# Other slots for the small tiles of the SSM, and its samples' transfers issued by POOL

## The chip, the cores and the metric

The kernel runs on one core of one Trainium2 chip. Its time is the device time of one execution in microseconds (us); several executions are timed and their median is given. In the profile, PE is TensorE (PEld its weight loads), DVE is VectorE, ACT is ScalarE, POOL is GpSimd and SP is SyncE. A suffix q, as in SPq, means that engine's sequencer, which issues DMAs and waits for semaphores.

## What is computed

One inference step of a hybrid decoder layer, in fp32, for one prompt of 1024 tokens with 16 meta tokens ahead of it and for 8 sample rows that each have a state of their own. Cut to what matters here:

```python
h = h + 0.5 * swiglu(rmsnorm(h, n1), w1g, w1u, w1d)
u = rmsnorm(h, nm) @ w_in
q, fz, iv, g, z, xbc, dt_raw = jnp.split(u, SPLITS, axis=-1)
# HGRN2: 4 heads of 128, a gated linear recurrence, S_t = diag(f_t) S_{t-1} + k_t v_t^T
o_hg, s_hg = run_segments(hgrn2_chunked, HG_CHUNK, segs, s_hg, silu(q), kk, iv, logf)
# Mamba-2 (SSM): 8 heads of 64, 2 groups, state 128; causal conv, then a chunked scan
xbc_act, conv_buf = causal_conv(xbc, s_conv, conv_w, conv_b)
dt = jax.nn.softplus(dt_raw + dt_bias)
#   per step: h_t = exp(dt_t A) h_{t-1} + dt_t x_t B_t^T ;  y_t = h_t C_t + D x_t
y, s_ssm = run_segments(functools.partial(ssd_chunked, a_neg=a_neg), SSM_CHUNK, segs, s_ssm, xs, dt, bm, cm)
mix = jnp.concatenate([o_hg, yz], axis=-1) @ w_out
h = h + mix
h = h + 0.5 * swiglu(rmsnorm(h, n2), w2g, w2u, w2d)
```

The outputs are the final norm of the prompt's and the samples' rows and all new states: SSM and HGRN states for the prompt, and for each of the 8 samples an SSM state (8 heads × 64 × 128, 256 KB) and an HGRN state (4 heads × 128 × 128).

## The kernel before

**Data and products.** Activations lie transposed: 128 partitions are features, the 1048 columns are tokens (1040 of the prompt, 8 samples). Every projection is made of three fp32r matmuls, high × high, high × low and low × high (`mm3`, L144 to L146). A weight tile of 128×512 is loaded raw by SP (`weights`, L126, from the pool "r"), its high part is made by ACT (L138) and its low part by DVE (L139).

**Stages in order.** FFN 1, with an order written out by hand; the mixer; FFN 2, by hand again. The mixer is `ssm_project` (projection, conv, and `ssm_decay` with the decays of all tokens), then the SSM scan and the SSM samples together, then four HGRN heads, each with projection, scan, samples and output, and the SSM gate (`ssm_gate`, L1263) and norm (`ssm_norm`, L1279, L1283) in between, then `out_proj`. In the mixer a scheduler decides the order of the instructions on each engine from the program's order and from which buffers are free; each engine then runs its list strictly in order. A DMA issue is an instruction in the list of the engine that issues it, so what stands behind a waiting issue waits too.

**Buffers.** `SLOTS = {"u": 30, "s": 8}`: 30 slots of kind "u" and 8 of kind "s", each 128×1056 fp32. `Pack` takes a slot and hands out pieces of it for small tiles. The pool "r" has 8 buffers of 128×512 for raw weights; the samples' states and rows take theirs from the same pool (`K.raw()`).

**The scan, `ssm_scan`.** Nine chunks (`CT`): eight of 128 tokens and one of 16. For each chunk c, three slots of kind "s" are taken. `mt` receives the cumulated decay of each head, broadcast over all partitions (`cumd`, L1118); ACT makes the decay matrix from it (Relu L1144, Exp L1145); DVE multiplies it with C·B (L1147). A pack `tk` holds `ec` (from `cumd` too, L1125), `bt` and `cbm`. `xx` holds x times dt and x times the decay. PE's L1151 gives the part inside the chunk, L1157 the part from the state; DVE adds them (L1158, L1159, L1162) and updates the state (L1170, L1171). Between the chunks' matmuls the scheduler places matmuls of the next projection. During the scan, four of the eight "s" slots belong to others: `K.st` (the small tiles of the decays), `ssm_samples`' `ex` and its `st`, and the pack of the state buffers.

**SSM samples, `ssm_samples`.** For each of 8 samples, SP loads the state (L1224, 512 rows of 512 B) and the row of B and C broadcast to 128 partitions (L1225, 128 rows of 2 KB). POOL multiplies the state with its decay (L1226) and adds the update in two halves (L1230, L1231). DVE reduces it with C (L1238, four), and SP stores the state (L1239). `skip` (L1249) closes the samples.

**HGRN samples.** In each head, twice four samples: load of the states and of v broadcast (L1492, L1493, by SP), three operations on POOL (L1494 to L1496), one matmul per sample on PE (L1499), and a store (L1500, by SP).

POOL's other DMAs are the seven small parameter loads at the start (L761).

Of the kernel before, what the change touches and what calls it, by code (L numbers as in the profile page):

```python
# [17 lines left out]
P = 128  # L18
D = 1024
KT = D // P  # L20
# [756 lines left out]
def constants_mix(K, a):  # L777
    nc = K.nc
    cst = K.const
    K.st = K.pack()  # L780

    K.tri = cst.tile([P, P], F32, name="tri")
    nc.gpsimd.affine_select(K.tri, K.ones[1], pattern=[[1, P]], compare_op=ALU.is_ge, fill=0.0, base=0, channel_multiplier=-1)

    K.mid = cst.tile([P, 32], U8, name="mid")
    for r in range(0, P, 32):
        nc.gpsimd.tensor_copy(K.mid[r : r + 32], K.ident[r : r + 32, r : r + 32])
    K.mask = {}
    for m in LEVELS[:5]:
        nb = 64 // m  # L790
        f = K.sml.tile([P, 64], F32, tag="mf", name=K.uid("mf"))
        fv = f.rearrange("p (b i) -> p b i", i=m)
        on = K.ones[1][:, :64].rearrange("p (b i) -> p b i", i=m)

        nc.gpsimd.affine_select(fv, on, pattern=[[-2 * m, nb], [0, m]], compare_op=ALU.is_ge, fill=0.0, base=0, channel_multiplier=1)
        nc.gpsimd.affine_select(fv, fv, pattern=[[2 * m, nb], [0, m]], compare_op=ALU.is_ge, fill=0.0, base=m - 1, channel_multiplier=-1)
        u = cst.tile([P, 16], U8, name=f"mask{m}")
        for r in range(0, P, 32):
            nc.gpsimd.tensor_copy(u[r : r + 32], f[r : r + 32, r // 2 : r // 2 + 16])
        K.mask[m] = u  # L800


    l0, l1 = K.pc["lb_logits"][:, 0:4], K.pc["lb_logits"][:, 4:8]
    e = K.st.tile([P, 12])
    nc.vector.tensor_max(e[:, 8:12], l0, l1)
    nc.vector.tensor_sub(e[:, 0:4], l0, e[:, 8:12])
    nc.vector.tensor_sub(e[:, 4:8], l1, e[:, 8:12])
    nc.scalar.activation(e[:, 0:8], e[:, 0:8], AF.Exp)
    nc.vector.tensor_add(e[:, 8:12], e[:, 0:4], e[:, 4:8])
    nc.vector.reciprocal(e[:, 8:12], e[:, 8:12])  # L810
    K.lb = cst.tile([P, 4], F32, name="lb")
    K.oml = cst.tile([P, 4], F32, name="oml")
    nc.vector.tensor_mul(K.lb, e[:, 0:4], e[:, 8:12])
    nc.vector.tensor_scalar(K.oml, K.lb, -1.0, 1.0, ALU.mult, ALU.add)

    K.dtb = K.st.tile([P, 8])
    nc.sync.dma_start(K.dtb, a["dt_bias"].to_broadcast([P, 8]))
    K.an = K.st.tile([P, 8])
    nc.sync.dma_start(K.an, a["a_log"].to_broadcast([P, 8]))
    nc.scalar.activation(K.an, K.an, AF.Exp)  # L820
    nc.vector.tensor_scalar_mul(K.an, K.an, -1.0)
    K.dcol = K.st.tile([P, 4])
    for hf in range(2):
        nc.sync.dma_start(K.dcol[64 * hf : 64 * hf + 64, :], a["d_skip"].rearrange("l (j f) -> f l j", f=2)[hf].to_broadcast([64, 4]))

    K.sel16 = cst.tile([16, 8], F32, name="sel16")
    s2 = K.sml.tile([16, 8], F32, tag="s2", name="s2", bufs=1)
    nc.gpsimd.affine_select(K.sel16, K.ones[1][:16, :8], pattern=[[-1, 8]], compare_op=ALU.is_equal, fill=0.0, base=0, channel_multiplier=1)
    nc.gpsimd.affine_select(s2, K.ones[1][:16, :8], pattern=[[-1, 8]], compare_op=ALU.is_equal, fill=0.0, base=-8, channel_multiplier=1)
    nc.gpsimd.tensor_add(K.sel16, K.sel16, s2)  # L830
# [137 lines left out]
def ssm_project(K, a, o):  # L968

    nc = K.nc  # L970
# [1 line left out]
    pc = K.pc  # L972


    rw = K.st.tile([P, KT, 8])
    nc.sync.dma_start(rw, wv[:, :, C_DT : C_DT + 8])
    wd = K.sml.tile([P, KT, 16], F32R, tag="wdt", name="wdt", bufs=1)
    nc.scalar.copy(wd[:, :, 0:8], rw)
# [14 lines left out]
    ps = K.psm()  # L993
    for k in range(8):
        nc.tensor.transpose(ps[:, 24 * k : 24 * k + 24], sc[:, k * P : (k + 1) * P], K.ident[:24, :24])
    sb = K.st.tile([P, 8, 8, 3])
    nc.vector.tensor_copy(sb.rearrange("p k b j -> p (k b j)"), ps[:, :192])

    K.xs = []
# [41 lines left out]
def ssm_decay(K, dtT):  # L1041

    nc = K.nc
# [2 lines left out]
    for c, (t0, n) in enumerate(CT):  # L1046
        nc.tensor.matmul(ps[:n, 8 * c : 8 * c + 8], dtT[:, t0 : t0 + n], K.sel16, start=True, stop=True)
    nc.tensor.matmul(ps[:8, 72:80], dtT[:, TP:T], K.sel16, start=True, stop=True)
    st = K.st

    def small(name):
        return st.tile([P, 80])

    K.dt = small("dt")
    x = small("dtx")
# [43 lines left out]

    pt = K.psm()  # L1100
    nc.tensor.transpose(pt[:72, :P], K.cum[:, 0:72], K.ident)
    ct = st.tile([72, P])
    nc.vector.tensor_copy(ct, pt[:72, :P])
    K.cumd = K.dram.tile([72, P], F32, name="cumd")
    nc.sync.dma_start(K.cumd, ct)
# [1 line left out]

def ssm_scan(K, a, o):
    nc = K.nc
    st = K.st  # L1110
    hts = K.pack()
    hbuf = [hts.tile([P, 512]) for _ in range(2)]
    xs, B, C = K.xs[0:4], K.xs[4:6], K.xs[6:8]
# [68 lines left out]
def ssm_samples(K, a, o):  # L1182

    nc = K.nc
    xs, B, C = K.xs[0:4], K.xs[4:6], K.xs[6:8]

    ex = K.pack()
    expd = ex.tile([8, 4, P])
    o8 = ex.tile([8, 512])
    nc.gpsimd.memset(o8, 1.0)  # L1190
    nc.gpsimd.affine_select(expd.rearrange("h j (f p) -> h j f p", f=2), o8.rearrange("h (j f p) -> h j f p", j=4, f=2), pattern=[[-2, 4], [-1, 2], [0, 64]], compare_op=ALU.is_equal, fill=0.0, base=0, channel_multiplier=1)
    st = K.pack()
    pd = K.psm()
    nc.tensor.transpose(pd[:8, 0:8], K.dt[:8, 72:80], K.ident[:8, :8])
    nc.tensor.transpose(pd[:8, 8:16], K.da[:8, 72:80], K.ident[:8, :8])
    dT = st.tile([8, 16])
    nc.vector.tensor_copy(dT, pd[:8, 0:16])
    pe = K.psm()
    for j in range(4):
        nc.tensor.matmul(pe[:, 16 * j : 16 * j + 16], expd[:, j], dT, start=True, stop=True)  # L1200
    pev = pe[:, 0:64].rearrange("p (j s b) -> p j s b", j=4, s=2)
    dec = st.tile([P, 4, 8])
    dx = st.tile([P, 4, 8])
    ys = st.tile([P, 4, 8])
    nc.scalar.activation(dec, pev[:, :, 1], AF.Exp)
    for j in range(4):
        nc.vector.tensor_mul(dx[:, j], pev[:, j, 0], xs[j][:, TP:T])
    pr = K.psm()
    for i in range(4):
        nc.tensor.transpose(pr[:8, i * P : (i + 1) * P], (B + C)[i][:, TP:T], K.ident)  # L1210
    br = st.tile([8, 512])
    nc.scalar.copy(br, pr[:8])
    bd = K.dram.tile([8, 512], F32, name="sbd")
    nc.sync.dma_start(bd, br)
    sv = a["state_ssm"].rearrange("l b (j f) p n -> l b (f p) j n", f=2)
    ov = o["ssm_sample"].rearrange("l b (j f) p n -> l b (f p) j n", f=2)

    state = {}

    def update(b):  # L1220
        sb = K.raw().rearrange("p (j n) -> p j n", j=4)
        rw = K.raw()
        rows = rw.rearrange("p (i n) -> p i n", i=4)
        nc.sync.dma_start(sb, sv[0, b])  # L1224
        nc.sync.dma_start(rw, bd[b : b + 1, :].to_broadcast([P, 512]))  # L1225
        nc.gpsimd.tensor_mul(sb, sb, dec[:, :, b : b + 1].broadcast_to([P, 4, P]))  # L1226
        for g in range(2):
            j2 = slice(2 * g, 2 * g + 2)
            up = K.t(2 * P).rearrange("p (j n) -> p j n", j=2)
            nc.gpsimd.tensor_mul(up, rows[:, g, None].broadcast_to([P, 2, P]), dx[:, j2, b : b + 1].broadcast_to([P, 2, P]))  # L1230
            nc.gpsimd.tensor_add(sb[:, j2], sb[:, j2], up)  # L1231
        state[b] = sb, rows

    def output(b):
        sb, rows = state.pop(b)
        junk = K.t(4 * P).rearrange("p (j n) -> p j n", j=4)
        for j in range(4):
            nc.vector.tensor_tensor_reduce(junk[:, j], sb[:, j], rows[:, 2 + j // 2], 1.0, 0.0, ALU.mult, ALU.add, ys[:, j, b : b + 1])  # L1238
        nc.sync.dma_start(ov[0, b], sb)  # L1239

    def sample(b):
        if b < NS:
            update(b)
        if b > 0:
            output(b - 1)

    def skip():
        for j in range(4):
            nc.vector.scalar_tensor_tensor(xs[j][:, TP:T], xs[j][:, TP:T], K.dcol[:, j : j + 1], ys[:, j], ALU.mult, ALU.add)  # L1249

    return [lambda b=b: sample(b) for b in range(NS + 1)] + [skip]
# [98 lines left out]
def hgrn_scan(K, a, o, hd, u):  # L1350

    nc = K.nc
# [136 lines left out]
    def samples(b0):  # L1489
        sb = K.raw().rearrange("p (b v) -> p b v", b=4)  # L1490
        vb = K.raw().rearrange("p (b v) -> p b v", b=4)
        nc.sync.dma_start(sb, a["state_hgrn"][0, b0 : b0 + 4, hd].rearrange("b k v -> k b v"))  # L1492
        nc.sync.dma_start(vb, vd[b0 : b0 + 4].partition_broadcast(P))  # L1493
        nc.gpsimd.tensor_mul(sb, sb, qs[:, 8 + b0 : 12 + b0, None].broadcast_to([P, 4, P]))  # L1494
        nc.gpsimd.tensor_mul(vb, vb, qs[:, 16 + b0 : 20 + b0, None].broadcast_to([P, 4, P]))
        nc.gpsimd.tensor_add(sb, sb, vb)  # L1496
        for i in range(4):
            b = b0 + i
            nc.tensor.matmul(po8[:, 16 + b : 17 + b], sb[:, i], qs[:, b : b + 1], start=True, stop=True)  # L1499
        nc.sync.dma_start(o["hgrn_sample"][0, b0 : b0 + 4, hd].rearrange("b k v -> k b v"), sb)  # L1500

    K.jobs += [lambda: samples(0), lambda: samples(4)]
    pieces.append((po8, 1024, 24))
# [423 lines left out]
```

## Time and profile before

| | us |
|---|---|
| median of three runs | 2042.24 |
| lowest and highest of them | 2039.06 and 2136.24 |
| the profiled execution, its time | 2041.44 |
| its span in the profile | 2039.7 |
| PE busy | 1962.5 (96%) |
| DVE busy | 1469.2 (72%) |
| ACT busy | 825.5 (40%) |
| POOL busy | 154.5 (8%) |

The profile is one execution, taken by the chip's profiler. Engines run side by side, so the shares do not add up to one. Busy shares are means over stages with different limits; the views by window and by wait tell what holds a given stage. The page's slices show where engines are busy, in tenths, in 40 slices of 51 us each; the scan lies in the 17th to 19th.

```profile
PE   6999999999999999979999999989999999999997
DVE  7777777777788586597453656877777777768973
POOL 3000000000002210231020111200000000000000
DMA  6233333335966621263120345224332333587851
```

### The profile page before, as it was taken

How to read it: one execution, taken by the hardware profiler on the slowest of the kernel's cores; microseconds unless marked ns; L12 is line 12 of the kernel's file. 1: busy time of each engine (PE TensorE's matmuls, PEld its weight loads, DVE VectorE, ACT ScalarE, POOL GpSimd, SP SyncE). 2: the span in 40 equal slices, each digit the busy share in tenths (PEclk: the TensorE clock that was granted, in tenths of full speed). 3: DMA queues.
4: the chain of work that ended last, by engine and by line, in shares of the span. 5: the costliest groups of instructions: out<-in, count | busy, mean ns of one | idle time of the engine just before them, and what ended most of it. 6: DMA issues, size and time to landing. Idle time of an engine off the chain costs nothing.

```text
span 2039.7 us, 40744 instructions
## 1 busy us (share of the span) xinstructions
PE 1962.5 (96%) x16647; PEld 1916.8 (94%) x16647; DVE 1469.2 (72%) x2439; ACT 825.5 (40%) x1530; POOL 154.5 (8%) x197
## 2 busy tenths in 40 slices
PE   6999999999999999979999999989999999999997
PEld 5999999999999999968989889989999999999997
DVE  7777777777788586597453656877777777768973
ACT  6522222223534553564534435742222222354352
POOL 3000000000002210231020111200000000000000
PEclk8999999999999999999999999999999999999999
DMA  6233333335966621263120345224332333587851
GB/s 212 76 103 90 101 104 94 96 94 179 315 211 213 183 82 33 90 189 92 50 75 11 107 124 182 72 70 113 93 109 80 103 102 96 161 239 238 265 176 61
DMA packets 323890, 259.32 MB, mean 127 GB/s; under 512 B 17584, under 2 KB 299440, under 8 KB 323696
## 3 DMA queue, kind: packets, MB, share of 16 engines
q1 hardware_dynamic: 323464, 256.68, 41.6%
q8 instruction: 131, 2.15, 0.4%
q14 instruction: 55, 0.45, 0.1%
q0 software_dynamic: 224, 0.04, 0.0%
q10 hardware_dynamic: 16, 0.00, 0.0%
HBM read 191.26 MB, written 65.47 MB: 126 GB/s over the span
## 4 chain that ended last, share of the span: by engine, by line
PE 82%; DVE 9%; DMA 3%; issue 2%; ACT 2%; SPq 0%; POOL 0%; DVEq 0%; ACTq 0%; POOLq 0%
PE acc L144 25%; PE acc L146 25%; PE acc L145 25%; DMA r<-in_w_ffn_up_dram 1%; DVE u L299 1%; DMA s<-in_x_prompt_dram 1%; DMA s<-cumd 1%; DVE ws L369 1%; PE mis L1462 0%; DVE u L578 0%; DVE t L449 0%; DVE ws L640 0%; PE mis L1420 0%; DVE s L664 0%; PE mis L1151 0%
## 5 line engine op out<-in xcount | busy, mean ns | idle before, releaser
L144 PE MATMUL acc<-u,ws 128*128 128x262 f32 (+2 forms) x4504 | 1321.1, 293 | 24.0 <-DVE t L463 6.5
L146 PE MATMUL acc<-u,ws 128*128 128x262 f32 (+2 forms) x4504 | 1316.3, 292 | 3.2 <-DVE ws L369 3.2
L145 PE MATMUL acc<-u,ws 128*128 128x262 f32 (+2 forms) x4504 | 1314.3, 292 | 4.2 <-DVE u L299 3.4
L144 PEld LDWEIGHTS acc<-u,ws 128*128 128x128 f32 x4504 | 857.7, 190 | 29.1 <-issue 10.4
L145 PEld LDWEIGHTS acc<-u,ws 128*128 128x128 f32 x4504 | 860.4, 191 | 8.2 <-DVE u L299 4.9
L146 PEld LDWEIGHTS acc<-u,ws 128*128 128x128 f32 x4504 | 855.4, 190 | 5.4 <-DVE ws L369 4.2
L369 DVE TENSOR_TENSOR ws<-r,ws 128x512 fp32r<-128x512 f32 x308 | 212.6, 691 | 78.8 <-ACT ws L365 78.7
L365 ACT CAST ws<-r 128x512 fp32r<-128x512 f32 x308 | 174.2, 616 | 4.9 <-DVE r L361 4.8
L484 ACT ACTIVATE t<-t 128x524 f32<-128x524 f32 x47 | 30.3, 645 | 305.8 <-DVE t L449 305.8
L361 DVE TENSOR_TENSOR r<-r,r 128x512 f32<-128x512 f32 x176 | 121.2, 691 | 13.2 <-DMA r<-in_w_ffn_up_dram 11.4
L205 POOL TENSOR_TENSOR t<-t,t 128x262 f32<-128x262 f32 x56 | 55.3, 998 | 778.8 <-ACT t L204 778.8
L461 ACT ACTIVATE t<-t 128x524 f32<-128x524 f32 x41 | 26.4, 644 | 204.5 <-DVE t L449 204.5
L578 DVE TENSOR_TENSOR u<-u,u 128x1048 fp32r<-128x1048 f32 (+1 forms) x84 | 97.8, 1167 | 9.2 <-ACT u L574 9.2
L139 DVE TENSOR_TENSOR ws<-r,ws 128x512 fp32r<-128x512 f32 x88 | 65.9, 759 | 42.4 <-ACT ws L138 42.1
L449 DVE TENSOR_TENSOR t<-t,u 128x524 f32<-128x524 f32 x135 | 91.0, 702 | 2.9
L664 DVE SCALAR_TENSOR_TENSOR s<-acc,s 128x524 f32<-128x524 f32 (+1 forms) x88 | 55.8, 650 | 41.5 <-PE acc L146 40.8
L574 ACT CAST u<-u 128x1048 fp32r<-128x1048 f32 (+1 forms) x84 | 83.4, 996 | 1.6 <-DMA u<-hd 1.6
L635 ACT CAST ws<-u 128x512 fp32r<-128x512 f32 (+1 forms) x72 | 42.2, 587 | 101.1 <-DVE u L630 93.1
L640 DVE TENSOR_TENSOR ws<-r,ws 128x512 fp32r<-128x512 f32 (+1 forms) x84 | 57.6, 698 | 31.0 <-ACT ws L635 31.0
L138 ACT CAST ws<-r 128x512 fp32r<-128x512 f32 x88 | 54.0, 618 | 55.0 <-PE acc L146 27.9
L635 ACT CAST ws<-r 128x512 fp32r<-128x512 f32 (+1 forms) x84 | 47.5, 582 | 70.1 <-DVE r L630 35.2
L454 ACT COPY t<-acc 128x524 f32<-128x524 f32 (+1 forms) x46 | 26.6, 579 | 106.0 <-PE acc L146 106.0
(381 smaller groups left out, 1897.8 us busy)
## 6 DMA issues: line engine op xcount, KB each, us to landing
hd<-s SPq DMA_DIRECT2D x170, 262.0 KB
u<-hd SPq DMA_DIRECT2D x64, 524.0 KB
r<-in_w_ffn_down_dram SPq DMA_DIRECT2D x128, 256.0 KB
r<-in_w_ffn_gate_dram SPq DMA_DIRECT2D x88, 256.0 KB
r<-in_w_ffn_up_dram SPq DMA_DIRECT2D x88, 256.0 KB
r<-in_w_in_dram SPq DMA_DIRECT2D x56, 256.0 KB
r<-in_w_ffn_down_dram SPq DMA_DIRECT2D x64, 192.0 KB
u<-hd SPq DMA_DIRECT2D x28, 393.0 KB
```

The source lines that it names most:

```text
L139: self.nc.vector.tensor_sub(lo, src, hi.bitcast(F32))
L144: mm(ps, whi, xhi, start=first, stop=False, skip_group_check=more)
L145: mm(ps, whi, xlo, start=False, stop=False, skip_group_check=more)
L146: mm(ps, wlo, xhi, start=False, stop=last, skip_group_check=more)
L361: self.K.nc.vector.tensor_tensor(self.raw[p], self.raw[x], self.raw[y], op)
L365: self.K.nc.scalar.copy(self.w[p][:, : self.n * P], self.raw[p])
L369: self.K.nc.vector.tensor_sub(t[:, 512 : 512 + w], self.raw[p], t[:, :w].bitcast(F32))
L449: nc.vector.tensor_mul(t, t if src is None else src, spread.lanes(i, cs))
L574: K.nc.scalar.copy(hi, lo.bitcast(F32))
L578: K.nc.vector.tensor_sub(lo, lo.bitcast(F32), hi.bitcast(F32))
L635: nc.scalar.copy(w[p, j, g][:, : n * P], src)
L640: nc.vector.tensor_sub(t[:, 512 : 512 + n * P], box[0], t[:, : n * P].bitcast(F32))
```

## The change

It has two parts. In the first, the small tiles of the SSM are divided anew. Those that live through the scan (`dt`, `dta`, `cum`, `wdec`, `ecl`, the biases, and the samples' `dT`, `dec`, `dx`, `ys`, `br`) share the one "s" slot of `K.st`. Those that are done before it (`e`, `rw`, `sb`, the steps of softplus, `last`, `ct`) go to a slot of kind "u", `K.st0`, and the samples' `ex` goes to another "u" slot. Six "s" slots are left for the chunks, where there were four. In the second, the loads and stores of the samples, of the SSM and of the HGRN heads, are issued by POOL: 24 DMAs in the scan and 6 in each head, 48 in all, of 256 KB each. SP has that many fewer in its list.

```diff
 def constants_mix(K, a):
-    K.st = K.pack()
+
+    K.st, K.st0 = K.pack(), K.pack("u")
...
-    e = K.st.tile([P, 12])
+    e = K.st0.tile([P, 12])
...
-    rw = K.st.tile([P, KT, 8])
+    rw = K.st0.tile([P, KT, 8])
...
-    sb = K.st.tile([P, 8, 8, 3])
+    sb = K.st0.tile([P, 8, 8, 3])
...
-    st = K.st
     def small(name):
-        return st.tile([P, 80])
+        return (K.st if name in ("dt", "dta", "cum", "wdec", "ecl") else K.st0).tile([P, 80])
...
-    ct = st.tile([72, P])
+    ct = K.st0.tile([72, P])
...
 def ssm_scan(K, a, o):
-    st = K.st
...
 def ssm_samples(K, a, o):
-    ex = K.pack()
+    ex = K.pack("u")
...
-    st = K.pack()
+    st = K.st
...
-        nc.sync.dma_start(sb, sv[0, b])
-        nc.sync.dma_start(rw, bd[b : b + 1, :].to_broadcast([P, 512]))
+        nc.gpsimd.dma_start(sb, sv[0, b])
+        nc.gpsimd.dma_start(rw, bd[b : b + 1, :].to_broadcast([P, 512]))
...
-        nc.sync.dma_start(ov[0, b], sb)
+        nc.gpsimd.dma_start(ov[0, b], sb)
...
     def samples(b0):
-        nc.sync.dma_start(sb, a["state_hgrn"][0, b0 : b0 + 4, hd].rearrange("b k v -> k b v"))
-        nc.sync.dma_start(vb, vd[b0 : b0 + 4].partition_broadcast(P))
+        nc.gpsimd.dma_start(sb, a["state_hgrn"][0, b0 : b0 + 4, hd].rearrange("b k v -> k b v"))
+        nc.gpsimd.dma_start(vb, vd[b0 : b0 + 4].partition_broadcast(P))
...
-        nc.sync.dma_start(o["hgrn_sample"][0, b0 : b0 + 4, hd].rearrange("b k v -> k b v"), sb)
+        nc.gpsimd.dma_start(o["hgrn_sample"][0, b0 : b0 + 4, hd].rearrange("b k v -> k b v"), sb)
```

## The prediction

> **What bounds the kernel now.** I read the page first.
>
> ```profile
> span 2039.7 us, 40744 instructions
> PE 1962.5 (96%) x16647; PEld 1916.8 (94%) x16647; DVE 1469.2 (72%) x2439; ACT 825.5 (40%) x1530; POOL 154.5 (8%) x197
> PE 82%; DVE 9%; DMA 3%; issue 2%; ACT 2%; SPq 0%; POOL 0%; DVEq 0%; ACTq 0%; POOLq 0%
> ```
>
> TensorE (PE) is busy for 96% of the span. The program still has the same matmuls after the change, so only PE's idle time can be won, or grow. The change sits in the SSM scan and the HGRN heads, so I cut that stretch into stages (busy us and count of PE, PEld, DVE, ACT, POOL; granted clock; DMA share; GB/s). The first row is the dense work before the scan, as a price list.
>
> ```profile
> 780.00:790.00 10.00, 10.00 (x65) 9.77 (x65) 5.75 (x26) 1.79 (x4) 0.00 (x0) 1.00 0.16 46
> 860.00:944.00 84.00, 72.90 (x515) 64.67 (x515) 72.41 (x182) 53.30 (x117) 26.68 (x34) 0.94 0.50 144
> 870.00:880.00 10.00, 8.87 (x64) 7.73 (x63) 10.00 (x20) 6.04 (x9) 5.67 (x7) 1.00 0.76 214
> 900.00:910.00 10.00, 3.64 (x19) 2.89 (x18) 10.00 (x31) 6.82 (x16) 1.62 (x3) 0.82 0.75 218
> 944.00:990.00 46.00, 41.42 (x662) 36.61 (x661) 27.88 (x53) 21.98 (x40) 10.36 (x8) 1.00 0.39 106
> 990.00:1085.00 95.00, 91.50 (x973) 85.93 (x972) 48.59 (x80) 41.39 (x78) 12.53 (x11) 1.00 0.21 61
> 1085.00:1160.00 75.00, 70.22 (x849) 66.32 (x849) 38.23 (x68) 29.20 (x57) 9.89 (x8) 1.00 0.27 79
> 1160.00:1240.00 80.00, 76.50 (x902) 72.40 (x901) 46.48 (x78) 37.70 (x68) 9.41 (x7) 0.98 0.39 126
> ```
>
> PE idles 84.00 − 72.90 = 11.1 us in the scan and 4.6, 3.5, 4.8 and 3.5 us in the four heads: 27.5 us in all, 1.3% of the span. That is the ceiling of any gain here. A gain of over 2% (41 us, about what a measurement of this kernel can tell from no change) would have to come from elsewhere. In the scan the vector engine (DVE) sets the pace: it is busy 10.00 of 10 us in two of the rows. Of the 11.1 us of PE's idle time, 6.4 lie in 900 to 910 alone.
>
> Next, the waits between 840 and 960 (engine, line, what ended the wait: us, times, longest):
>
> ```profile
> ACT s L1144 <- DMA s<-cumd: 8.6, 5, 3.8
> SPq L1239 <- POOL r L1231: 8.4, 4, 3.3
> SPq L1500 <- POOL r L1496: 3.9, 1, 3.9
> ```
>
> SP issues every load. It stands at L1239, the store of a sample's state, until POOL has finished that sample. Everything behind it on SP stands too. SP's own sequence shows whom this hits.
>
> ```profile
> 856.54 0.39 SPq L1239 DMA_DIRECT2D out_dram<-r  x1
> 857.03 0.46 SPq L1118 DMA_DIRECT2D s<-cumd  x1
> 901.40 0.38 SPq L1239 DMA_DIRECT2D out_dram<-r  x1
> 901.82 0.51 SPq L126 DMA_DIRECT2D r<-in_w_in_dram  x1
> 958.88 0.38 SPq L1500 DMA_DIRECT2D out_dram<-r  x1
> 959.36 5.05 SPq L126 DMA_DIRECT2D r<-in_w_in_dram  x7
> ```
>
> Chunk 1's load of `cumd` (857.03) and two batches of weights (901.82, 959.36) leave right behind such a store. The chain that ended last runs through such loads, at these places and in head 2:
>
> ```profile
> 857.03 4.12 DMA s<-cumd
> 903.12 3.58 DMA s<-cumd
> 959.36 3.28 DMA r<-in_w_in_dram
> 1134.91 3.53 DMA r<-in_w_in_dram
> ```
>
> **The change, part by part.** The sum is made against the profiled execution's own 2041.44 us (span 2039.7 and 1.7 us around it). That execution is 0.8 us below the median of the three runs, 2042.24, so I treat them as one.
>
> *1. Six slots instead of four for the chunks.* A chunk takes three slots: the decay tile, the pack and `xx`. With four slots only one chunk fits whole. With six, chunk c+1's load and its Relu and Exp on ACT can go ahead while chunk c is worked on. In the order of the changed program, SP issues the `cumd` loads of chunks 1 and 2 with no sample's store ahead of them. That takes the 4.12 us leg at 857.03 off the path. As DVE is full there, not all of it turns into PE time; I count it in step 3.
>
> *2. Small tiles in other slots.* `K.st0` and `ex` now sit in two of the 30 "u" slots. The PE order outside the scan and head 0 is the same, instruction for instruction, so nothing there waits for another slot by the program. Cost 0, hidden by the "u" slots being returned before the heads need them; bounds −1 to +1 us.
>
> *3. Samples' DMAs to POOL, in the scan.* Twenty-four DMAs of 256 KB go from SP to POOL: eight state loads and eight stores with 512 rows of 512 B, and eight row broadcasts with 128 rows of 2 KB. SP's queue loses its stands at L1239. POOL pays the issues. Its work per sample now:
>
> ```profile
> L1226 POOL TENSOR_TENSOR r<-r,s 128x512 f32<-128x512 f32 x8 | 8.7, 1087 | 89.6 <-ACT s L1205 72.6 <-DVE s L1147 10.3 <-DVE u L1309 4.5
> L1230 POOL TENSOR_TENSOR t<-r,s 128x256 f32<-128x256 f32 x16 | 12.0, 770 | 10.6 <-DVE s L1147 10.6
> L1231 POOL TENSOR_TENSOR r<-r,t 128x256 f32<-128x256 f32 x16 | 11.8, 759 | 0.0
> 2.93 0.54 POOL L761 DMA_DIRECT2D t<-in_conv_w_dram  x1
> 4.00 0.52 POOL L761 DMA_DIRECT2D t<-in_hg_norm_dram  x1
> t<-in_hg_norm_dram POOLq DMA_DIRECT2D x1, 2.0 KB, 6.2
> 853.61 1.53 POOL L1230 TENSOR_TENSOR t<-r,s 128x256 f32<-128x256 f32 x2 [10.60 <-DVE s L1147]
> 899.86 1.51 POOL L1231 TENSOR_TENSOR r<-r,t 128x256 f32<-128x256 f32 x2
> 914.29 0.69 DVE L1158 TENSOR_TENSOR s<-mis,s 128x512 f32<-128x512 f32 x1 [4.19 <-PE mis L1157]
> ```
>
> Tensor work is 1.09 + 2 × 0.77 + 2 × 0.76 = 4.15 us a sample. The only issues by POOL in the trace are small: 0.52 us for 4 rows, 0.54 for 32. The difference is 0.7 ns a row; carried on, 512 rows cost 0.88 and 128 rows 0.61. This is an estimate far outside its rows. The bound below is 0.52, no cost by rows. The bound above is the 6.2 us that a POOL-issued transfer took to land, if POOL had to stand until then; I don't go near that end, since POOL was through with the issue at 2.93 after 0.54 us; the rivals take in part of it.
>
> With the estimate a sample holds POOL for 4.15 + 2 × 0.88 + 0.61 = 6.5 us. The scan's nine chunks take 84 us, 9.3 each, so POOL still keeps up. Counted from 853.6, eight samples end at 905.8, where the last one now ends at 899.86 + 1.51 = 901.4. So the samples end 4.4 us later. Now what waits for them: in the changed order DVE's outputs of samples 6 and 7 (L1238) stand ahead of chunk 5's L1158. Four outputs take 1.2 us, and chunk 5 resumes at about 907.0 where it now does so at 914.29: PE then has its gate weights, which no longer sit behind the store at 901.40. The scan's rest, 914.3 to 944, takes 29.7 us as before; it ends at 936.7, 7.3 us earlier. But fewer matmuls lie in it. In the orders of the two programs 312 projection matmuls lie inside the scan before and 283 after. Those 29 now run in head 0 at 10.00/65 = 0.154 us each, 4.5 us. Net −2.8 us. That is the term; its bounds are −8.0 (6.4 of idle time at 900 to 910 and 1.6, a third of the scan's other 4.7, for three chunks of nine whose loads come earlier, with nothing given back) and the first rival's price.
>
> *4. Samples' DMAs to POOL, in the heads.* The last sample work and its reader in head 0, and ssm_norm's sum on POOL:
>
> ```profile
> 957.23 1.62 POOL L1496 TENSOR_TENSOR r<-r,r 128x512 f32<-128x512 f32 x1
> 985.76 1.40 PE L1499 MATMUL mis<-qs,r 128*128 128x1 f32 x12
> 1068.22 2.42 POOL L1279 TENSOR_TENSOR s<-s,s 128x1048 f32<-128x1048 f32 x1 [12.00 <-ACT s L1278]
> ```
>
> Six DMAs a head leave SP. SP's stands at L1500 go, and with them up to 3.28 + 3.53 = 6.8 us of the two weight loads on the chain. Against that, a weight's buffer is one of the eight "r" buffers that the samples use too, and comes free only when POOL's store has landed, later than SP's. I take −1.5 us; bounds −6.8 and +2. The +2 is for head 2, where in the changed order POOL's load stands, with its wait for a buffer, ahead of L1279, on which PE's L1283 waits; I take no more than one L1279, 2.4 us, less a little that PE fills. POOL's own lateness costs nothing in the heads: head 0's samples are done at 958.8, and PE's L1499 reads them from 985.8.
>
> *5. Contention.* Two rows of one operation on DVE:
>
> ```profile
> 897.25 0.29 DVE L1238 CUSTOM_DVE_ANT_0 t<-r,r 128x128 f32<-128x128 f32 x1
> 897.67 1.13 DVE L1238 CUSTOM_DVE_ANT_0 t<-r,r 128x128 f32<-128x128 f32 x1
> ```
>
> It takes 0.29 us where POOL is still idle and 1.13 beside POOL's tensor work, 0.84 us more. POOL's 24 issues of the scan could do the same: at most 24 × 0.84 = 20 us of DVE, at least 0. An issue reads no tile and I put it near the low end: +1.5 us.
>
> Sum: 2041.4 + 0 − 2.8 − 1.5 + 1.5 = 2038.6 us.
>
> **The rivals.**
>
> *POOL becomes the pace.* If DVE, which streams without a gap in 870 to 880 and 900 to 910, holds up POOL's issues by the same factor as POOL holds up L1238 (1.13/0.29 = 3.9), a sample costs 4.15 + 2 × 3.4 + 2.4 = 13.4 us. Eight end at 960.8, the scan at 960.8 + 1.2 + 29.7 = 991.7, 47.7 us later; with the 4.5 us of moved matmuls this gives 2093. At a factor of 2, 1.76 and 1.2 us an issue, a sample takes 8.9 us, the samples end at 924.8 and the scan at 955.7: +11.7 + 4.5, 2058. It decides from the point where samples end about 2.8 us later than I have it, 0.35 us a sample. For it: the L1238 rows and a full DVE. Against it: POOL's tensor work, which does read tiles, runs at 0.77 us in the same window. [...]
>
> *A transfer waits for the one before.* If a large issue by POOL must wait until room is free, that is until the transfer before has landed, only part of the landing shows, as POOL's 4.15 us of work lies between. A state load by SP shows how long that is:
>
> ```profile
> 861.04 0.50 SPq L1224 DMA_DIRECT2D r<-in_state_ssm_dram  x1
> 865.79 1.05 POOL L1226 TENSOR_TENSOR r<-r,s 128x512 f32<-128x512 f32 x1 [1.42 <-DMA r<-in_state_ssm_dram]
> ```
>
> Issued at 861.04, it released POOL at 865.79, after 4.75 us; less 4.15 of work that is 0.6 us a sample and I say 1, since the row loads wait too. At 1 us a sample the samples end 8 us later: 2038.6 + 8 = 2047.
>
> *The waits go and nothing takes their place.* All of step 3's −8.0 and step 4's −6.8: 2041.4 − 14.8 = 2026.6. For it: POOL was busy for only 26.7 of the scan's 84 us. Against it: DVE is full.
>
> *It doesn't do what it says.* DVE's pace holds the scan as it is and the heads' loads wait for "r" buffers anyway: 2041 to 2042.
>
> **How the numbers follow.** My forecast, 2033 to 2044, has a chance of 0.48; it covers the case of no effect, to which I give 0.12 more. The wait for landing, 2044 to 2052, has 0.15. POOL as the pace, 2052 to 2093, has 0.15, and by its rows half of that lies above 2082.6, which is 2% over 2041.4. The full gain has 0.10. The range from 2027 to 2064 leaves out the far end of POOL's case (0.1) and what little lies below. Faster by over 2% would need more than all idle time of the stages, 0.01; slower by over 2%: 0.08; within: 0.91.
>
> **What would show it.** Right: `cumd` waits of ACT well under 8.6 us; no SP stand at a store; POOL issue rows of about 0.9 and 0.6 us; samples done near 906; scan's last chunk near 936; PE idle in 900 to 910 smaller, and about 29 more matmuls in head 0. Wrong: POOL issue rows above 1.5 us, or DVE idle at L1238 with POOL as the releaser, puts the time above 2050. A gain that comes with PE idle in the heads under 2 us each would be the full gain.

## The result, and the profile after

The changed kernel takes 2060.5 us (median of four runs, 2057.2 to 2064.35) against 2040.65 (four runs). The ratio is 1.0100, with a 95% interval of 1.0081 to 1.0119: 20 us or 1% slower, within 2%, but clear of noise. One execution of the kernel before took 2136.24 us, in a slower state of the chip, and is left out of the ratio. The forecast was 2.8 us faster. The time lies in the range given, near its far end, where the rivals were. The profiled execution of the changed kernel took 2057.2 us. In it, lines from about L1050 on have a number lower by one.

The head of its page:

```profile
span 2055.4 us, 40746 instructions
PE 1967.1 (96%) x16647; PEld 1919.5 (93%) x16647; DVE 1472.1 (72%) x2439; ACT 826.6 (40%) x1532; POOL 184.4 (9%) x245
PE 82%; DVE 9%; issue 3%; DMA 3%; ACT 2%; POOL 1%; SPq 0%; DVEq 0%; ACTq 0%; POOLq 0%
```

No engine has more work to speak of; POOL has 30 us more, the issues among them, and appears on the chain that ended last. The windows of the scan (busy us and count of PE, PEld, DVE, ACT, POOL; granted clock; DMA share; GB/s) show PE's idle time:

```profile
850.00:860.00 10.00, 7.94 (x50) 7.65 (x48) 3.73 (x4) 9.23 (x22) 4.88 (x8) 1.00 0.56 166
860.00:870.00 10.00, 4.21 (x25) 3.36 (x26) 6.45 (x18) 1.41 (x2) 5.24 (x8) 0.66 0.50 135
870.00:880.00 10.00, 6.27 (x42) 5.83 (x40) 7.77 (x14) 7.62 (x17) 7.20 (x10) 0.99 0.57 155
900.00:910.00 10.00, 6.26 (x51) 5.22 (x50) 9.39 (x22) 6.10 (x15) 7.11 (x10) 1.00 0.39 101
910.00:920.00 10.00, 7.74 (x49) 6.51 (x48) 5.66 (x19) 4.04 (x8) 3.68 (x5) 0.87 0.74 214
920.00:930.00 10.00, 5.35 (x27) 4.53 (x27) 7.87 (x24) 6.13 (x16) 3.68 (x6) 0.67 0.61 179
```

In these six windows PE idles 22.2 us. Before, it idled 9.0 in the same six. Two of them stand in the prediction, these are two more, and in 850 to 860 and 910 to 920 it did not idle:

```profile
860.00:870.00 10.00, 8.52 (x63) 7.81 (x63) 8.13 (x22) 8.80 (x22) 8.58 (x11) 1.00 0.98 292
920.00:930.00 10.00, 10.00 (x80) 9.23 (x80) 9.45 (x20) 8.70 (x21) 0.00 (x0) 1.00 0.16 28
```

DVE, which was busy for all of 870 to 880 and 900 to 910 before, has gaps there now. PE's granted clock is lower as well, 0.66 and 0.67 in 860 to 870 and 920 to 930 where it was 1.00; what that adds, no run separates. What DVE, ACT and POOL waited for in the scan (engine, line, releaser: us, times, longest):

```profile
DVE t L1237 <- POOL r L1230: 15.5, 4, 6.5
POOL r L1223 <- issue: 14.6, 5, 6.2
ACT ws L138 <- DMA r<-in_w_in_dram: 13.8, 3, 9.3
POOL out_dram L1238 <- issue: 4.7, 2, 3.4
```

POOL stands for 14.6 + 4.7 = 19.3 us ahead of its large DMA issues, and "issue" means that the trace names no releaser. DVE's outputs (L1237) wait for the late POOL, and all that stands behind them on DVE waits too. Before, DVE never waited there. POOL's own sequence shows the stands in the brackets (start, duration, engine, line, then the idle time before and its releaser):

```profile
846.64 0.59 POOL L1224 DMA_DIRECT2D r<-sbd  x1 [7.04 <-DVE s L1146]
847.62 0.76 POOL L1223 DMA_DIRECT2D r<-in_state_ssm_dram  x1 [0.39 <-issue]
848.37 0.54 POOL L1224 DMA_DIRECT2D r<-sbd  x1
855.10 0.76 POOL L1223 DMA_DIRECT2D r<-in_state_ssm_dram  x1 [6.19 <-issue]
865.02 0.81 POOL L1238 DMA_DIRECT2D out_dram<-r  x1 [0.57 <-POOL r L1225]
870.24 0.75 POOL L1223 DMA_DIRECT2D r<-in_state_ssm_dram  x1 [4.41 <-issue]
917.56 0.76 POOL L1238 DMA_DIRECT2D out_dram<-r  x1 [3.42 <-issue]
921.37 1.41 POOL L1230 TENSOR_TENSOR r<-r,t 128x256 f32<-128x256 f32 x2
```

An issue itself is short, 0.54 to 0.81 us. But the third state load stands 6.2 us behind two row loads and a state load that were issued just ahead of it; the next one stands 4.4 us behind two stores and a row load. The last sample ends at 922.8, where it ended at 901.4 before.

The landings in the same trace say what POOL stands for. The issue at 855.10 comes 0.33 us after the state load of 847.62 has landed (854.77), the one at 870.24 comes 0.34 us after the store of 865.02 (869.90), the one at 917.56 comes 0.31 us after the load of 912.84 (917.25), and the other three stands of over 1 us without a releaser end so too. Two more stands ahead of L1223, of 2.3 us each, are put down to DVE in the view, but they also end 0.31 and 0.34 us after a store of POOL's has landed; with them the samples' stands are 23.9 us.

PE's last steps of the scan and the heads come later throughout. The transposes that close the scan ran at 943.35 before and run at 954.54. Where the 29 moved matmuls went can be read between two points of head 0, `ssm_norm`'s first sum and the output norm, before and after:

```profile
978.30 0.54 PE L1283 MATMUL mis<-s,ones 128*128 128x350 f32 x1
987.47 0.68 PE L1518 MATMUL mis<-s,ones 128*128 128x512 f32 x1
```

```profile
990.28 0.54 PE L1282 MATMUL mis<-s,ones 128*128 128x350 f32 x1
1004.13 0.68 PE L1517 MATMUL mis<-s,ones 128*128 128x512 f32 x1
```

The lag is 12.0 us at the first and 16.7 at the second, so the moved matmuls cost 4.7. From there to the end of the heads it stays between 16 and 19 us, and the spans differ by 15.7.

### The profile page after: what moved, and what is told of

Its sections match the earlier page's. It is cut to its first block, busy times and chain, and to the rows that moved or that the text cites. A ratio compares the mean times of both kernels' runs of the same rounds, so it can differ in the third digit from the quotient of the medians.

```text
span 2055.4 us, 40746 instructions
## 1 busy us (share of the span) xinstructions
PE 1967.1 (96%) x16647; PEld 1919.5 (93%) x16647; DVE 1472.1 (72%) x2439; ACT 826.6 (40%) x1532; POOL 184.4 (9%) x245
## 4 chain that ended last, share of the span: by engine, by line
PE 82%; DVE 9%; issue 3%; DMA 3%; ACT 2%; POOL 1%; SPq 0%; DVEq 0%; ACTq 0%; POOLq 0%
PE acc L144 25%; PE acc L146 25%; PE acc L145 25%; DVE u L299 1%; DMA s<-in_x_prompt_dram 1%; DMA r<-in_w_ffn_up_dram 1%; PE mis L1419 1%; DVE ws L369 0%; PE mis L1517 0%; PE mis L1461 0%; DVE u L578 0%; DVE ws L640 0%; DVE s L664 0%; DVE t L449 0%; PE mis L1479 0%
```

## The experiments

Three theories stood at the start. Theory 1, room: POOL stands until its earlier transfers have left room for the next one; the room is taken to be what `dynamic_dma_scratch_size` sets in the program, 1024 bytes. Theory 2, starvation: DVE's streaming holds POOL's issues up. Theory 3, order: the scan's new order of instructions costs the time. Each ratio below is against the kernel before on the same chip, with its 95% interval; 0.1% is 2 us. The kernel before had medians of 2039.4 to 2043.5 in these sets, so ratios are compared, not times.

**Twice the room.**

```diff
-    nc = _bacc.Bacc("TRN2", target_bir_lowering=False, num_devices=1, dynamic_dma_scratch_size=1024)
+    nc = _bacc.Bacc("TRN2", target_bir_lowering=False, num_devices=1, dynamic_dma_scratch_size=2048)
...
-        f = K.sml.tile([P, 64], F32, tag="mf", name=K.uid("mf"))
+        f = K.sml.tile([P, 64], F32, tag="mf", name=K.uid("mf"), bufs=1)
...
-    vs8 = small("vs8", 8, P)
+    vs8 = small("kt8", 16, P)[:8]
```

> [...] The room is found by letting vs8 share the buffer of kt8 and one mask tile have one buffer; the order of instructions on every engine is that of the changed kernel. Theory 1, room: POOL stands ahead of its large DMA issues (14.6 us ahead of L1223 and 4.7 ahead of L1238 in the scan, with no releaser in the trace) because its earlier transfers still fill the room; with twice the room these stands fall under 6 us in all, the last sample ends about 15 us earlier, DVE's 15.5 us of waiting at L1237 falls under 5, and the time falls by 10 to 16 us, to 2043 to 2050. Theory 2, starvation: DVE's streaming holds POOL's issues up; the stands stay and the time stays at 2057 to 2064. Theory 3, order: the new order of the scan costs the time; stands may go, but the time moves by less than 4 us.

Measured: 2047.12 us, ratio 1.0045 (1.0031 to 1.0059). Of the 20 us, 11 to 14 are gone, against the changed kernel and against the control below. No stand of POOL's without a releaser is left among its waits in the scan. POOL's sequence at the same place as above and its last sample, then a wait of DVE's, then chunk 5's L1157 on DVE:

```profile
849.67 0.76 POOL L1223 DMA_DIRECT2D r<-in_state_ssm_dram  x1
850.42 0.54 POOL L1224 DMA_DIRECT2D r<-sbd  x1
851.00 0.76 POOL L1223 DMA_DIRECT2D r<-in_state_ssm_dram  x1
905.56 1.54 POOL L1230 TENSOR_TENSOR r<-r,t 128x256 f32<-128x256 f32 x2
```

```profile
DVE t L1237 <- POOL r L1230: 4.5, 2, 3.9
```

```profile
912.59 0.69 DVE L1157 TENSOR_TENSOR s<-mis,s 128x512 f32<-128x512 f32 x1 [0.18 <-PE mis L1156]
```

The third state load now follows at once. The last sample ends at 907.1, 15.7 us earlier. DVE waits 4.5 us for POOL instead of 15.5. The order of PE and DVE is that of the changed kernel, so theory 3 is out for this part. DVE is busy for 9.96 to 10.00 us in each 10 us from 870 to 910, and yet the stands are gone, so theory 2 is out for them too.

**A control for the shared buffers.** The same edit with 1024 bytes.

```diff
-        f = K.sml.tile([P, 64], F32, tag="mf", name=K.uid("mf"))
+        f = K.sml.tile([P, 64], F32, tag="mf", name=K.uid("mf"), bufs=1)
...
-    vs8 = small("vs8", 8, P)
+    vs8 = small("kt8", 16, P)[:8]
```

> A control for the kernel with twice the room: the same sharing of buffers (vs8 with kt8, one mask tile), the room as in the changed kernel, 1024 bytes. By every theory 2057 to 2064; if it were faster by 5 us or more, the sharing and not the room would have made the difference.

Measured: 2064.23 us, 1.0115 (1.0094 to 1.0135), as the changed kernel. The room made the difference.

**Less room.**

```diff
-    nc = _bacc.Bacc("TRN2", target_bir_lowering=False, num_devices=1, dynamic_dma_scratch_size=1024)
+    nc = _bacc.Bacc("TRN2", target_bir_lowering=False, num_devices=1, dynamic_dma_scratch_size=640)
```

> [...] Theory 1: room for one large transfer only, so that a row load, too, waits for a large one; the stands in the scan more than double (over 40 us), the last sample ends 20 us later or more, and the time is 2075 to 2100. Starvation by DVE: no change, 2057 to 2064.

Measured: 2082.97 us, 1.0206 (1.0176 to 1.0236). Its waits in the scan:

```profile
DVE t L1237 <- POOL r L1230: 38.3, 4, 12.3
POOL out_dram L1238 <- issue: 13.1, 4, 3.9
POOL r L1224 <- issue: 12.2, 6, 3.6
POOL r L1223 <- issue: 6.2, 2, 3.4
```

The stands without a releaser sum to 31.5 us. Six more, 18.5 us in all, are put down to a load of `cumd`, to ACT or to DVE, but end 0.30 to 0.31 us after a transfer of POOL's has landed, as the others do; with them it is 50 us, over the 40 that I had expected. Now the small row loads (L1224) stand as well. So with 640, 1024 and 2048 bytes the kernel is 2.1%, 1.0 to 1.15% and 0.45% slower than before: the time follows the room.

**The same bytes in a quarter of the rows.**

```diff
-    sv = a["state_ssm"].rearrange("l b (j f) p n -> l b (f p) j n", f=2)
+    sv = a["state_ssm"].rearrange("l b h (p q) n -> l b (h p) (q n)", q=4)
...
-        nc.gpsimd.dma_start(sb, sv[0, b])
+        nc.gpsimd.dma_start(sb, sv[0, b].rearrange("p (j n) -> p j n", j=4))
```

(and the same for the output)

> [...] It leaves out the right placing of the state's elements in the tile, so the samples' SSM outputs are of other elements; all else is as in the changed kernel, in the same order. Theory 1, room for descriptors: the stands ahead of L1223 and L1238 go (under 2 us in all) with the room of 1024 bytes, and the time falls to 2040 to 2050, at least as far as with twice the room. A rival, that POOL stands until earlier bytes have landed, or that DVE starves it: the stands keep at least half of their 19 us and the time stays above 2053.

Measured: 2048.07 us, 1.0038 (1.0025 to 1.0051), with the room at 1024 bytes. POOL's sequence has no stand left at that place, and a large issue takes some 0.54 us instead of 0.76:

```profile
850.46 0.54 POOL L1223 DMA_DIRECT2D r<-in_state_ssm_dram  x1
851.03 0.54 POOL L1224 DMA_DIRECT2D r<-sbd  x1
851.57 0.54 POOL L1223 DMA_DIRECT2D r<-in_state_ssm_dram  x1
```

As many bytes and as many DMAs, and the stands are gone, though the state loads land no sooner (median 4.8 us after the issue, against 3.9 in the changed kernel and 5.0 with twice the room). What fills up goes by the rows, not the bytes. Ahead of 855.10 three transfers with 128 + 512 + 128 = 768 rows were under way, and the next one, with 512, did not go; with 2048 bytes, at the same place, it did. The traces agree: counted in rows, with the landings, no issue of POOL's in the changed kernel begins with more than 768 on the way, its own included, and every one that would have made it 1024 or more waited. With 640 bytes, 512 went through and 640 waited; with 2048, 1792 went through. What it is of a row that takes the room, a descriptor as the expectation has it or something else, no run shows.

**Both remedies.**

```diff
-    sv = a["state_ssm"].rearrange("l b (j f) p n -> l b (f p) j n", f=2)
+    sv = a["state_ssm"].rearrange("l b h (p q) n -> l b (h p) (q n)", q=4)
...
-    nc = _bacc.Bacc("TRN2", target_bir_lowering=False, num_devices=1, dynamic_dma_scratch_size=1024)
+    nc = _bacc.Bacc("TRN2", target_bir_lowering=False, num_devices=1, dynamic_dma_scratch_size=2048)
```

(and the other lines of the two edits)

> [...] It asks whether the 8 us by which each remedy alone stays slower than before are still the room. If the room: under 2044. If they are POOL's own 2 us of issues a sample, its slower landings and the scan's order, which neither remedy touches: 2044 to 2050, as with either alone.

Measured: 2047.87 us, 1.0031 (1.0017 to 1.0045), as with either. So the rest, 6 to 9 us, isn't the room.

**The parts of the change alone.** Slots only:

```diff
-        nc.gpsimd.dma_start(sb, sv[0, b])
+        nc.sync.dma_start(sb, sv[0, b])
```

(and so for all six kinds of the samples' DMAs)

> The slots of the change, with all 48 transfers of the samples issued by SP as before. Theories 1 and 2, POOL's issues cost the time: not slower than before, 2032 to 2042. Theory 3, the new order with six slots costs it: 2050 or more.

POOL only, the opposite edit on the kernel before:

> The slots of before, with all 48 transfers issued by POOL. Theories 1 and 2: slower than before by 10 us or more, 2050 to 2062, with stands ahead of POOL's issues in the scan as in the changed kernel. Theory 3: within 4 us of before.

Measured: slots only 2040.99 us, 1.0009 (0.9997 to 1.0021); POOL only 2056.57 us, 1.0083 (1.0068 to 1.0098). The slots cost or bring nothing that can be measured, and POOL's DMAs carry nearly all of it, with either slots. In the run with POOL only, POOL also stands ahead of L1224 to L1239 with no releaser, for 22.3 us in all.

**The scan and the heads apart.** The changed kernel with the heads' DMAs by SP:

```diff
-        nc.gpsimd.dma_start(sb, a["state_hgrn"][0, b0 : b0 + 4, hd].rearrange("b k v -> k b v"))
+        nc.sync.dma_start(sb, a["state_hgrn"][0, b0 : b0 + 4, hd].rearrange("b k v -> k b v"))
```

(and so for the heads' row loads and stores)

> The changed kernel with the transfers of the HGRN heads issued by SP again; PE, DVE and ACT have the order of the changed kernel. If POOL's issues cost in the scan alone (theories 1 and 2 with the heads' slack): within 3 us of the changed kernel, 2055 to 2063. If the heads gained by the move, as predicted (1.5 us), it is slower by that; if the heads lose by it, it is faster by over 3 us.

Measured: 2061.83 us, 1.0107 (1.0091 to 1.0122): as the changed kernel. With twice the room besides:

> Twice the room, with the SSM samples' transfers by POOL and the heads' by SP. It places the 6 us by which twice the room stays slower than before. If they lie in the scan (POOL's own issues ahead of its work, its slower landings): 2044 to 2050, as with the heads on POOL. If they come from the heads: 2038 to 2043.

Measured: 2049.97 us, 1.0045 (1.0029 to 1.0061), the same ratio as with the heads on POOL. So the rest comes with the SSM samples' transfers. And the heads alone on POOL, with the slots:

> The slots of the change with the HGRN heads' transfers alone by POOL (24 DMAs, 6 a head) and the scan's by SP. Step 4 of the prediction gave the heads −1.5 us with bounds of −6.8 and +2. If it holds: 2 us under the kernel with the slots alone, 2037 to 2041. If POOL's slower landings or its room cost in the heads too: 2043 or more.

Measured: 2044.18 us, 1.0020 (1.0009 to 1.0032), against 1.0009 with the slots alone. The two intervals overlap. No gain of the heads is found, and they may lose 2 us.

The profiles tell more of where the time goes. The scan is taken from PE's L1200 just ahead of it (L1199 where lines are lower by one) to the transposes that close it, and head 0 between the two points shown above, all in us:

| | L1200 | closing transposes | scan | head 0 |
|---|---|---|---|---|
| before | 840.59 | 943.35 | 102.8 | 9.2 |
| changed kernel | 837.18 | 954.54 | 117.4 | 13.9 |
| slots only | 837.63 | 941.15 | 103.5 | 13.0 |
| changed, twice the room | 839.60 | 942.79 | 103.2 | 13.9 |
| changed, rows of 2 KB | 840.41 | 943.34 | 102.9 | 13.8 |

Either remedy takes 14 us off the scan and makes it as long as with the slots alone. The rest is therefore not to be seen in the scan, and these single executions do not show where else it is. The moved matmuls come mostly with the slots: between the two points there are 34 projection matmuls before, 58 with the slots alone and 63 in the changed kernel.

**Are SP's stands worth anything?** Each SSM store one sample later in the program, by SP:

```diff
-        nc.sync.dma_start(ov[0, b], sb)
+        late.append(lambda: nc.sync.dma_start(ov[0, b], sb))
...
         if b < NS:
             update(b)
+        if late and b > 0:
+            late.pop(0)()
...
     def skip():
+        late.pop(0)()
```

> The slots of the change, all DMAs by SP, and each SSM sample's store written one sample later in the program, so that SP should no longer stand at L1238 until POOL is through. It tests the step of the prediction that the removal of SP's stands is worth time in the scan. If it is: SP's 17 us of waits at the store fall under 6 and the time is 2030 to 2037, below both kernels. If DVE's pace hides them: within 3 us of the kernel with the slots alone (2041).

> The kernel before with the same later store and its own slots. If SP's stands are what chunk 1's cumd load and the weights at 902 wait for: 2032 to 2037. If DVE's pace hides them: 2037 to 2043.

Measured: 2042.72 us, 1.0001 (0.9988 to 1.0014), with the new slots; 2043.76 us, 1.0004 (0.9988 to 1.0020), with the old. With the new slots the edit did only part of what it should: SP's waits at the store went from 17.1 to 12.9 us, not under 6. With the old slots the waits behind POOL's L1231 fall from 8.4 to 3.0 us, and the last store's, 6.5 before, stays:

```profile
SPq L1239 <- POOL t L1393: 6.7, 1, 6.7
SPq L1239 <- POOL r L1231: 3.0, 1, 3.0
```

The time did not move. A stronger edit leaves seven of the eight stores out:

```diff
-        nc.sync.dma_start(ov[0, b], sb)
+        if b == NS - 1:
+            nc.sync.dma_start(ov[0, b], sb)
```

> The slots of the change, all DMAs by SP, and seven of the eight stores of the SSM samples left out (only the last one is made). It bounds from above what SP's stands at L1238, and the buffers held until a store has landed, can cost. If they cost what the prediction's step 3 supposed: 2028 to 2036. If DVE's pace hides them: 2037 to 2042.

Measured: 2042.84 us, 1.0009 (1.0000 to 1.0019), the ratio of the slots alone. SP's waits in the scan, first with the slots alone, then without the stores:

```profile
SPq L1238 <- POOL r L1230: 17.1, 5, 5.0
SPq L126 <- DVE s L1237: 4.8, 3, 3.1
```

```profile
SPq L126 <- DVE s L1237: 18.3, 3, 8.4
SPq L1223 <- DVE s L1237: 18.1, 3, 9.0
```

The stands at the stores are gone, but SP now stands ahead of the next loads, until DVE's outputs are through with the buffers that these take. ACT waits 14.2 us for `cumd`, against 8.1 with the slots alone, and the time is the same. So these stands can move and grow without a cost, and taking away those at the stores wins nothing. What a scan would gain in which SP never stood, this run does not bound.

**Stores alone on POOL.** The kernel before with L1239 and L1500 by POOL.

```diff
-        nc.sync.dma_start(ov[0, b], sb)
+        nc.gpsimd.dma_start(ov[0, b], sb)
```

> The kernel before, with its slots, and the stores of the samples alone (L1239, L1500: 8 in the scan, 2 a head) issued by POOL; loads stay with SP. SP no longer stands at a store. Theory 1: with one large transfer of POOL's at a time the room never fills, POOL pays 0.8 us a sample, and the waits of the scan that stood behind SP's stores go: 2030 to 2040, the prediction's step 3 and 4 without its price. If SP's stands cost nothing in the scan because DVE sets its pace: within 3 us of before. Starvation: slower by 3 us or more.

Measured: 2053.49 us (nine runs, 2046.67 to 2062.83), 1.0062 (1.0043 to 1.0081), slower by 13 us. The times expected of theory 1 and of hidden stands were both missed. Only the number expected of starvation is met, but the issues still take 0.75 to 0.88 us, so that isn't shown either. Two of its waits, then a row of POOL and two of DVE:

```profile
POOL out_dram L1239 <- issue: 7.2, 3, 3.2
PE mis L1151 <- DVE s L1147: 17.6, 3, 8.2
```

```profile
882.09 0.80 POOL L1239 DMA_DIRECT2D out_dram<-r  x1 [1.74 <-issue]
```

```profile
875.28 5.22 DVE L1162 SCALAR_TENSOR_TENSOR u<-u,s,s 128x128 f32<-128x128 f32 x4
882.56 6.06 DVE L1147 TENSOR_TENSOR s<-s,s 128x512 f32<-128x512 f32 x2
```

POOL stands ahead of single stores too, for 7.2 us in all; each follows the one before by 3 to 8 us. The three stands end 0.3 to 0.4 us after the store before has landed, which agrees with two large transfers, 1024 rows, not fitting together. Besides, the samples' work on POOL falls on other instructions of DVE than before: four of L1162 take 5.22 us and two of L1147 6.06, where two of L1147 took 1.28 to 1.80 before. An issue of POOL's falls into each of these times, but so does its tensor work, and the order on PE differs from that of the kernel before. How the 13 us divide between stands, contention and order is open.

**POOL's time without the transfers.**

```diff
             up = K.t(2 * P).rearrange("p (j n) -> p j n", j=2)
+            for _ in range(4 - g):
+                nc.gpsimd.memset(up, 0.0)
```

> The slots of the change, all DMAs by SP, and seven small memsets of a scratch tile ahead of each SSM sample's products on POOL, about 2.2 us a sample: as much of POOL's time as its three issues take in the changed kernel, with none of their transfers. It asks what the 6 us in the scan are that twice the room leaves. If it is POOL's time: 2045 to 2051. If it is the slower landing of POOL's transfers, which loads and weights wait for: 2038 to 2044.

Measured: 2045.82 us, 1.0020 (1.0008 to 1.0031). That is some 2 us more than the slots alone, with intervals that overlap, where twice the room leaves 7. The absolute range that was expected is met at its lower edge, but by the ratio POOL's time explains a minor part. The scheduler also ordered the scan anew for it, so this is an indication, not proof. What is left, some 5 us, stays open; slower landings are the candidate that was only argued. With twice the room, POOL's row loads took 4.9 us from issue to landing (median); before, a row load of SP's issued at 849.84 had landed when POOL went on at 853.61, 3.8 us later.

No version tried here is faster than the kernel before.

## Why the prediction was wrong

*What bounds the kernel* held as far as it says that DVE sets the scan's pace. Its own consequence was not drawn: if DVE is full, SP's stands can be hidden. The reading "right behind a store, and on the chain, so the store costs" took the chain for a price. Without seven stores SP stands for DVE instead, and the ratio is that of the slots alone.

*Step 1*, that the `cumd` leg would leave the path: right in the profile of the changed kernel (ACT's wait for it falls from 8.6 to 3.4 us), but not by the slots, as the step's title has it. With the slots alone the wait is 8.1 us. With twice the room it is 4.4, and the scan is no shorter for it (103.2 us against 103.5).

*Step 2*, other slots at no cost: right within 0.2%.

*Step 3* failed, in two terms.
- The issue's price was nearly right: 0.88 and 0.61 us were worked out from rows of 4 and 32, and 512 and 128 rows take 0.75 to 0.81 and 0.54 to 0.63. But POOL's time per sample was taken as work plus issues, with no stand. The bound of 6.2 us was set aside because POOL was through with an issue of 32 rows after 0.54 us; but POOL's seven loads there have 72 rows together, and in the changed kernel 768 on the way still went through. The stands are 19.3 us, 23.9 with the two put down to DVE, the last sample ended at 922.8 and not 905.8, and DVE's outputs and the weights' buffers waited with it, DVE for 15.5 us: the prediction's own sign that the time would be above 2050. This is the step that turned the sign, with 11 to 14 of the 20 us.
- The gain of 7.3 us took it that chunk 5 resumes as soon as the last outputs are through. With twice the room the samples end at 907.1, nearly as predicted, and yet chunk 5's L1157 comes at 912.6 and the scan's last transposes at 942.8 instead of 943.35: 0.6 us earlier, not 7.3; counted from L1200, the scan is 0.4 us longer. So the gain was not there. PE's idle time at 900 to 910 does fall, from 6.4 to 1.0 us, but PE idles 4.9 us at 860 to 870 (1.5 before) and 3.4 at 910 to 920 (none before). The moved matmuls, 4.5 us predicted and 4.7 measured, then come on top, mostly by the slots and not by the DMAs.

*Step 4*, the heads at −1.5 us: no gain was found (1.0107 without the move, 1.0100 with it; 1.0020 with it alone against 1.0009), but so small a one is within these intervals. That a store of POOL's lands later than one of SP's is not shown: POOL's took 2.7 to 6.5 us in the scan, and the trace gives no landing of SP's stores. The 6.8 us of loads on the chain were not to be had.

*Step 5*, contention by issues: most keep their length beside a full DVE. A store's issue in the changed kernel, and the window around it:

```profile
883.13 0.76 POOL L1238 DMA_DIRECT2D out_dram<-r  x1
```

```profile
880.00:890.00 10.00, 8.66 (x50) 7.45 (x51) 9.89 (x18) 1.65 (x3) 8.21 (x12) 0.67 0.47 153
```

DVE is busy for 9.89 of the 10 us, and the issue takes 0.76. DVE's operations beside these issues are mostly products of two inputs. The longest issues of the samples stand beside DVE operations with one tensor input, L1307 and L1308, of 0.8 us: a state load of 1.30 us from 896.20 with the heads by SP, a store of 1.07 from 900.74 with twice the room, and a row load of 0.95 from 888.22 with rows of 2 KB, which end 0.30, 0.31 and 0.12 us after that operation. So DVE may hold an issue up beside such an operation, but by half a us at most, and it is not what the 20 us are.

*The rivals.* "A transfer waits for the one before" had the mechanism, but priced it at 8 us where the stands cost 11 to 14. It let one transfer stand at a time and hid it behind 4.15 us of work. In fact two or three loads are issued in a row, and the wait is for the room of several; that it ends with a landing was right. "POOL becomes the pace" had the price, 2058, by another cause: it doubled the issue for starvation, and what came was the stand.

## What to carry to other kernels

Before DMAs are moved to POOL, count rows, not bytes: add up the rows of all transfers that will be in flight at once. Here, at 1024 bytes, 768 went through, and 1024 or more stood. In these runs a stand for room shows in the trace as an idle POOL ahead of its own DMA (6.2 us ahead of 855.10), with no releaser or with one that has nothing to do with it; it ends 0.3 to 0.4 us after an earlier DMA of POOL's has landed, and everything behind it in POOL's order is late. And before a queue's wait is priced as a gain, ask whether the pace is set elsewhere: leave the waited-for work out, and see in the trace whether the wait is gone or only stands at the next thing.

## What the runs showed of the hardware

A POOL-issued DMA of 256 KB holds POOL for some 0.54 us with 128 rows of 2 KB and 0.76 with 512 rows of 512 B, but with `dynamic_dma_scratch_size` at 1024 the next one can stand 6.2 us, until 0.3 us after an earlier one has landed; at 2048 there was no such stand. POOL's and DVE's operations can take far longer beside each other than I had taken from L1238. In the run with the stores on POOL, two products of DVE took 6.06 us for 1.28, and one of POOL's, beside a DVE without a gap, took 6.38 us for a mean of 1.41 in the kernel before; that the one slows the other is the near reading, and no run isolates it:

```profile
919.31 6.38 POOL L1494 TENSOR_TENSOR r<-r,qs 128x512 f32<-128x512 f32 x1 [20.17 <-DMA r<-in_state_hgrn_dram]
```
